# Grouped instance norm on one core: gamma's load and columns rebuilt, an early write and 60 no-ops removed

## The chip, the cores and the metric

The kernel runs on one core of one Trainium2 chip. The metric is the device time of one execution in microseconds (us); before the change its median is 626.75 us over 3 runs (626.71 to 626.87). The core has five engines that run side by side, each with its own instruction stream: TensorE (PE, with its weight loads shown as PEld), VectorE (DVE), ScalarE (ACT), GpSimd (POOL) and SyncE (SP). Transfers between the chip's main memory (HBM) and the on-chip memory (SBUF) are carried by 16 DMA engines. SyncE, ScalarE and GpSimd each issue transfers into a queue of their own; the 16 engines serve all queues.

## The reference

```python
def reference(x, gamma):                       # x: 4 x 8 x 16 x 256 x 256, gamma: 8 x 16
    mu = x.mean(axis=(3, 4), keepdims=True)
    var = ((x - mu) ** 2).mean(axis=(3, 4), keepdims=True)
    x_norm = (x - mu) / np.sqrt(var + 1e-5)
    out = x_norm * gamma[None, :, :, None, None]
    return out.astype(np.float32)
```

There are 4 x 8 x 16 = 512 channels of 65,536 numbers. Each is normalized by its own mean and variance and multiplied by one number of gamma. 134 MB are read and 134 MB are written.

## The kernel before

A channel is cut into S = 8 pieces of F = 8192 numbers, and a tile holds K = 16 channels: 128 partitions (8 neighbouring ones belong to a channel) by 8192 numbers, 4 MB. There are U = 32 tiles, and gamma repeats every NG = 8 tiles. Six slots of SBUF (AHEAD = 6, `xt`) hold tiles; each is loaded, normalized in place and stored from the same slot. So load u + 6 has to wait until store u has landed.

The order on each engine is the order of the code. The loads of the first six tiles are issued at once, tiles 1 and 3 on ScalarE's queue and 0, 2, 4 and 5 on SyncE's (lines 56 and 57). Later loads are SyncE's (line 136), all 32 stores are ScalarE's (line 134).

For a tile (lines 105 to 136) VectorE sums every partition (line 107) and ScalarE squares with a running sum (line 108); both wait for the load. One matmul with the constant matrix `navg` adds the 8 partitions of a channel, scales by -1/65536, and gives every partition of the channel the result (line 116, `ps`; in 4-byte floats it runs as two halves). VectorE forms the negative variance (`nvar`, line 117), ScalarE the root (`std`, line 121), VectorE the reciprocal (`rstd`, line 125) and its product with gamma (`scale`, line 127), which reads a column of `g_col`; then VectorE normalizes the tile (line 130), and ScalarE issues the store.

The column `g_col` has to hold, for each of the 8 tile kinds, gamma's value of each partition. Before the change it is made ahead of the loop. Gamma is loaded as one row of 128 numbers on one partition (`g_row`, line 55, GpSimd's queue). VectorE repeats each number 8 times (`g_rep`, line 83), 8 matmuls with a single 1 as the other operand turn the row into 8 columns (`g_ps`, line 88), and VectorE copies them to SBUF (line 94).

Three more things stand ahead of the loop. VectorE zeroes a small tile `touch`, and GpSimd's queue writes it to 16 rows of the output, 512 bytes each, in the place of tile 0 (lines 53 and 54); store 0 later overwrites it. ScalarE gets 60 no-ops behind its two loads (lines 59 and 60). A root over a constant (`root_eps`, line 78) has ScalarE load its table of functions early.

Of the kernel before, what the change touches and what calls it, by code (L numbers as in the profile page):

```python
# [1 line left out]

# [4 lines left out]

F32 = mybir.dt.float32
U8 = mybir.dt.uint8
ALU = mybir.AluOpType  # L10
ACTF = mybir.ActivationFunctionType
AX = mybir.AxisListType


@with_exitstack
def kernel(
    ctx: ExitStack,
    tc: tile.TileContext,
    x: bass.AP,
    gamma: bass.AP,  # L20
    out: bass.AP,
):
    nc = tc.nc
    B, G, C, H, W = x.shape
    P = nc.NUM_PARTITIONS
    HW = H * W
    n_ch = B * G * C
    S = 8
    K = P // S
    F = HW // S  # L30
    U = n_ch // K
    NG = (G * C) // K
    AHEAD = 6
    assert HW % S == 0 and (G * C) % K == 0

    xv = x.rearrange("b g c h w -> (b g c h w)").rearrange("(u p f) -> u p f", p=P, f=F)
    ov = out.rearrange("b g c h w -> (b g c h w)").rearrange("(u p f) -> u p f", p=P, f=F)
    gv = gamma.rearrange("g c -> (g c)")

    data = ctx.enter_context(tc.tile_pool(name="data", bufs=1))  # L40
    singles = ctx.enter_context(tc.tile_pool(name="singles", bufs=1))
    psum = ctx.enter_context(tc.tile_pool(name="psum", bufs=4, space=bass.MemoryType.PSUM))
    ctx.enter_context(tc.manual_schedule())

    slots = [data.tile([P, F], F32, name=f"xt{i}") for i in range(AHEAD)]

    def load(u, queue):
        queue.dma_start(out=slots[u % AHEAD][:], in_=xv[u])  # L48


    g_row = singles.tile([1, G * C], F32, name="g_row")
    touch = singles.tile([16, 128], F32, name="touch")
    nc.vector.memset(touch[:], 0.0)  # L53
    nc.gpsimd.dma_start(out=ov[0][0::S, 0:128], in_=touch[:])  # L54
    nc.gpsimd.dma_start(out=g_row[:], in_=gv[None, :])  # L55
    for u in range(AHEAD):
        load(u, nc.scalar if u in (1, 3) else nc.sync)

    for _ in range(60):
        nc.scalar.nop()  # L60

    eps_t = singles.tile([P, 1], F32, name="eps_t")
    nc.gpsimd.memset(eps_t[:], 1e-5)
    one = singles.tile([1, 1], F32, name="one")
    nc.gpsimd.memset(one[:], 1.0)
    navg = singles.tile([P, K, S], F32, name="navg")
    nc.gpsimd.memset(navg[:], -1.0 / HW)  # L67
    nc.gpsimd.affine_select(  # L68
        out=navg[:], in_=navg[:], pattern=[[-S, K], [0, S]], compare_op=ALU.is_ge,
        fill=0.0, base=0, channel_multiplier=1,  # L70
    )
    nc.gpsimd.affine_select(  # L72
        out=navg[:], in_=navg[:], pattern=[[S, K], [0, S]], compare_op=ALU.is_ge,
        fill=0.0, base=S - 1, channel_multiplier=-1,
    )
    navg_w = navg[:].rearrange("p k s -> p (k s)")
    root_eps = singles.tile([P, 1], F32, name="root_eps")
    nc.scalar.activation(out=root_eps[:], in_=eps_t[:], func=ACTF.Sqrt)  # L78
    g_rep = singles.tile([1, NG, K, S], F32, name="g_rep")
    g_ps = psum.tile([P, NG], F32, name="g_ps", bufs=1)  # L80
    g_col = singles.tile([P, NG], F32, name="g_col")

    nc.vector.tensor_copy(  # L83
        out=g_rep[:],
        in_=g_row[:].rearrange("o (n k) -> o n k", n=NG).unsqueeze(3).to_broadcast([1, NG, K, S]),
    )
    for n in range(NG):
        nc.tensor.matmul(  # L88
            out=g_ps[:, n : n + 1],
            lhsT=g_rep[:, n].rearrange("o k s -> o (k s)"),  # L90
            rhs=one[:],
            start=True, stop=True,
        )
    nc.vector.tensor_copy(out=g_col[:], in_=g_ps[:])  # L94

    junk = singles.tile([P, F], U8, name="junk")

    st = singles.tile([P, U, 2], F32, name="st")
    nvar = singles.tile([P, U], F32, name="nvar")
    std = singles.tile([P, U], F32, name="std")  # L100
    rstd = singles.tile([P, U], F32, name="rstd")
    scale = singles.tile([P, U], F32, name="scale")

    squares = []
    for u in range(U):
        t = slots[u % AHEAD]
        nc.vector.reduce_sum(out=st[:, u, 0:1], in_=t[:], axis=AX.X)  # L107
        square = nc.scalar.activation(  # L108
            out=junk[:], in_=t[:], func=ACTF.Square, accum_out=st[:, u, 1:2],
        )  # L110
        if u:

            tc.declare_no_dep(square.ins, squares[-1].ins, reason="junk, ordered by the root between")
        squares.append(square)
        ps = psum.tile([P, 2], F32, name="ps")
        nc.tensor.matmul(out=ps[:], lhsT=navg_w, rhs=st[:, u], start=True, stop=True)  # L116
        nc.vector.tensor_scalar(  # L117
            out=nvar[:, u : u + 1], in0=ps[:, 0:1], scalar1=ps[:, 0:1],
            scalar2=ps[:, 1:2], op0=ALU.mult, op1=ALU.add,
        )  # L120
        nc.scalar.activation(  # L121
            out=std[:, u : u + 1], in_=nvar[:, u : u + 1], func=ACTF.Sqrt,
            bias=eps_t[:], scale=-1.0,
        )
        nc.vector.reciprocal(out=rstd[:, u : u + 1], in_=std[:, u : u + 1])  # L125
        g = u % NG
        nc.vector.tensor_mul(  # L127
            out=scale[:, u : u + 1], in0=rstd[:, u : u + 1], in1=g_col[:, g : g + 1],
        )
        nc.vector.tensor_scalar(  # L130
            out=t[:], in0=t[:], scalar1=ps[:, 0:1], scalar2=scale[:, u : u + 1],
            op0=ALU.add, op1=ALU.mult,
        )
        nc.scalar.dma_start(out=ov[u], in_=t[:])
        if u + AHEAD < U:
            load(u + AHEAD, nc.sync)


# [1 line left out]
_INS = ['x', 'gamma']  # L140
_OUTS = [((4, 8, 16, 256, 256), 'float32')]


# [23 lines left out]
```

## Time and profile before

| what | value |
|---|---|
| median of the runs | 626.75 us (3 runs, 626.71 to 626.87) |
| span of the profiled execution | 624.9 us |
| HBM read, written | 134.22 MB, 134.23 MB, together 430 GB/s over the span |
| packets of the DMA engines | 9282, of which 1072 under 512 bytes |
| VectorE, sum of a tile (L107) | 8685 ns each, 32 times |
| VectorE, normalize a tile (L130) | 4550 ns each, 32 times |
| ScalarE, squares of a tile (L108) | 7030 ns each, 32 times |
| TensorE, half a matmul of the sums (L116) | 349 ns each, 64 |
| VectorE, repeat gamma (L83), copy the columns (L94) | 681 ns, 166 ns, once each |
| TensorE, half a matmul of gamma (L88) | 347 ns each, 16 |
| store, from issue to landing (L134) | 62.5 us median |
| load on SyncE's queue, on ScalarE's queue (L48) | 38.5 us, 31.5 us median |
| early write (L54), gamma's load (L55) | 9.1 us, 13.3 us |

The span is the time from the first to the last instruction that the profiler recorded in one execution; the runs' time has something around it. A row of a group of instructions gives how often it ran and how long one took. The time to landing counts from the issue of a transfer until its completion is signalled, the time in the queue behind others included. A chain of waits is followed back from the last instruction: at each step to what released it. In a table by stretches the times are counted from the start of the span, and the DMA share is the mean busy share of the 16 engines, where a packet counts in the stretch in which it starts. No-ops don't appear among the recorded instructions.

### The profile page before, as it was taken

The numbers are of one execution on the slowest core, as the hardware profiler recorded it, in microseconds if no ns is written. First come the engines' busy times: TensorE is split into PE (matmuls) and PEld (weight loads), VectorE is DVE, ScalarE is ACT, GpSimd is POOL, SyncE is SP. The second block draws the span as 40 slices with busy tenths as digits, with TensorE's granted clock in tenths as the row PEclk, the third lists the DMA queues.
The fourth block names the chain that finished last, engine by engine and source line by source line (L and its number), as shares of the span: only waits on it lengthen the run. The fifth ranks groups of instructions, "written<-read, shape, count | busy, mean of one in ns | idle before, by whom it ended". The sixth has DMA issues, their size and how long they took to land.

```text
span 624.9 us, 631 instructions
## 1 busy us (share of the span) xinstructions
PE 21.4 (3%) x80; PEld 19.5 (3%) x80; DVE 443.4 (71%) x163; ACT 238.8 (38%) x98; POOL 2.4 (0%) x11
## 2 busy tenths in 40 slices
PE   0200000000000000000000000000000000000000
PEld 0200000000000000000000000000000000000000
DVE  0588999999776687666786767867668676687730
ACT  0444444444443234432344423444224442244400
POOL 1000000000000000000000000000000000000000
DMA  8999999999999999999999999999999999999998
GB/s 370 436 426 430 422 434 436 436 436 437 432 424 433 436 436 424 436 436 434 436 436 432 422 436 436 434 426 436 436 434 436 436 434 419 436 436 434 426 436 369
DMA packets 9282, 268.46 MB, mean 430 GB/s; under 512 B 1072, under 2 KB 1088, under 8 KB 1088
## 3 DMA queue, kind: packets, MB, share of 16 engines
q10 hardware_dynamic: 4896, 142.61, 52.9%
q1 hardware_dynamic: 4320, 125.83, 46.8%
q0 software_dynamic: 64, 0.01, 0.0%
q14 instruction: 2, 0.02, 0.0%
HBM read 134.22 MB, written 134.23 MB: 430 GB/s over the span
## 4 chain that ended last, share of the span: by engine, by line
another core or an unknown queue 61%; DMA 17%; DVE 15%; SPq 1%; PE 1%; issue 0%; ACT 0%
DVE st L107 10%; DMA xt<-in_x_dram 10%; DMA out_dram<-xt 8%; DVE xt L130 5%; SPq L48 1%; PE ps L116 1%; ACT std L121 0%; DVE nvar L117 0%; DVE rstd L125 0%; DVE scale L127 0%
## 5 line engine op out<-in xcount | busy, mean ns | idle before, releaser
L107 DVE TENSOR_REDUCE st<-xt 128x1 f32<-128x8192 f32 x32 | 277.9, 8685 | 100.4 <-DMA xt<-in_x_dram 100.4
L108 ACT ACTIVATE junk<-xt 128x8192 uint8<-128x8192 f32 x32 | 225.0, 7030 | 275.1 <-DMA xt<-in_x_dram 231.9
L130 DVE TENSOR_SCALAR xt<-xt,ps,scale 128x8192 f32<-128x8192 f32 x32 | 145.6, 4550 | 1.2
L121 ACT ACTIVATE std<-nvar,eps_t 128x1 f32<-128x1 f32 x32 | 9.4, 294 | 79.6 <-DVE nvar L117 79.6
L116 PE MATMUL ps<-st,navg 128*128 128x2 f32 x64 | 17.9, 349 | 557.1 <-DVE st L107 557.1
L116 PEld LDWEIGHTS ps<-st,navg 128*128 128x128 f32 x64 | 16.0, 311 | 558.9 <-issue 558.9
L117 DVE TENSOR_SCALAR nvar<-ps 128x1 f32<-128x1 f32 x32 | 9.2, 287 | 23.8 <-PE ps L116 23.8
L125 DVE RECIPROCAL rstd<-std 128x1 f32<-128x1 f32 x32 | 5.2, 164 | 11.6 <-ACT std L121 11.6
L83 DVE COPY g_rep<-g_row 1x1024 f32<-1x1024 f32 x1 | 0.7, 681 | 14.3 <-DMA g_row<-in_gamma_dram 14.3
L108 ACT ACTIVATION_READ_ACCUMULATOR junk<-xt 128x1 f32 x32 | 6.0, 186 | 0.0
L127 DVE TENSOR_TENSOR scale<-rstd,g_col 128x1 f32<-128x1 f32 x32 | 5.1, 159 | 1.1
L88 PE MATMUL g_ps<-one,g_rep 1*128 1x1 f32 x16 | 3.5, 347 | 16.1 <-DVE g_rep L83 16.1
L88 PEld LDWEIGHTS g_ps<-one,g_rep 1*128 1x128 f32 x16 | 3.5, 325 | 16.1 <-issue 16.1
L94 DVE COPY g_col<-g_ps 128x8 f32<-128x8 f32 x1 | 0.2, 166 | 3.7 <-PE g_ps L88 3.7
L78 ACT ACT_TABLE_LOAD x1 | 1.3, 1283 | 1.7 <-PEq L151 1.7
L53 DVE MEMSET touch<- 16x128 f32 x1 | 0.2, 165 | 0.9 <-PEq L151 0.9
L54 POOL DMA_DIRECT2D out_dram<-touch x1 | 0.6, 619 | 0.8 <-DVE touch L53 0.8
L55 POOL DMA_DIRECT2D g_row<-in_gamma_dram x1 | 0.5, 487 | 0.0
L68 POOL TENSOR_SCALAR_AFFINE_SELECT navg<-navg 128x128 f32<-128x128 f32 x1 | 0.4, 400 | 0.1
L72 POOL TENSOR_SCALAR_AFFINE_SELECT navg<-navg 128x128 f32<-128x128 f32 x1 | 0.4, 399 | 0.1
L67 POOL MEMSET navg<- 128x128 f32 x1 | 0.2, 232 | 0.0
L78 ACT ACTIVATE root_eps<-eps_t 128x1 f32<-128x1 f32 x1 | 0.2, 203 | 0.0
(6 smaller groups left out, 0.6 us busy)
## 6 DMA issues: line engine op xcount, KB each, us to landing
out_dram<-xt ACTq DMA_DIRECT2D x32, 4096.0 KB, 62.5
xt<-in_x_dram SPq DMA_DIRECT2D x30, 4096.0 KB, 38.5
xt<-in_x_dram ACTq DMA_DIRECT2D x2, 4096.0 KB, 31.5
out_dram<-touch POOLq DMA_DIRECT2D x1, 8.0 KB, 9.1
g_row<-in_gamma_dram POOLq DMA_DIRECT2D x1, 0.5 KB, 13.3
```

The source lines that it names most:

```text
L48: queue.dma_start(out=slots[u % AHEAD][:], in_=xv[u])
L78: nc.scalar.activation(out=root_eps[:], in_=eps_t[:], func=ACTF.Sqrt)
L83: nc.vector.tensor_copy(out=g_rep[:], in_=g_row[:].rearrange("o (n k) -> o n k", n=NG).unsqueeze(3).to_broadcast([1, NG, K, S]),)
L88: nc.tensor.matmul(out=g_ps[:, n : n + 1], lhsT=g_rep[:, n].rearrange("o k s -> o (k s)"), rhs=one[:], start=True, stop=True,)
L107: nc.vector.reduce_sum(out=st[:, u, 0:1], in_=t[:], axis=AX.X)
L108: square = nc.scalar.activation(out=junk[:], in_=t[:], func=ACTF.Square, accum_out=st[:, u, 1:2],)
L116: nc.tensor.matmul(out=ps[:], lhsT=navg_w, rhs=st[:, u], start=True, stop=True)
L117: nc.vector.tensor_scalar(out=nvar[:, u : u + 1], in0=ps[:, 0:1], scalar1=ps[:, 0:1], scalar2=ps[:, 1:2], op0=ALU.mult, op1=ALU.add,)
L121: nc.scalar.activation(out=std[:, u : u + 1], in_=nvar[:, u : u + 1], func=ACTF.Sqrt, bias=eps_t[:], scale=-1.0,)
L125: nc.vector.reciprocal(out=rstd[:, u : u + 1], in_=std[:, u : u + 1])
L127: nc.vector.tensor_mul(out=scale[:, u : u + 1], in0=rstd[:, u : u + 1], in1=g_col[:, g : g + 1],)
L130: nc.vector.tensor_scalar(out=t[:], in0=t[:], scalar1=ps[:, 0:1], scalar2=scale[:, u : u + 1], op0=ALU.add, op1=ALU.mult,)
```

## The change

Gamma is loaded as it lies in memory, 8 rows of 16 numbers (64 bytes) on 8 partitions, by ScalarE's queue between loads 1 and 3. GpSimd issues no transfer any more. The early write with its memset and the 60 no-ops are gone. GpSimd makes an 8 x 8 unit matrix `eye` in place of the single 1. Within the loop, behind the sum of tile 0 on VectorE, the rows are repeated 8 times each (8 partitions x 128 numbers), one matmul with the unit matrix gives all 8 columns at once, and VectorE copies them.

```diff
@@ -48,21 +47,21 @@
-    g_row = singles.tile([1, G * C], F32, name="g_row")
-    touch = singles.tile([16, 128], F32, name="touch")
-    nc.vector.memset(touch[:], 0.0)
-    nc.gpsimd.dma_start(out=ov[0][0::S, 0:128], in_=touch[:])
-    nc.gpsimd.dma_start(out=g_row[:], in_=gv[None, :])
+
+    g_rows = singles.tile([NG, K], F32, name="g_rows")
     for u in range(AHEAD):
         load(u, nc.scalar if u in (1, 3) else nc.sync)
-
-    for _ in range(60):
-        nc.scalar.nop()
+        if u == 1:
+            nc.scalar.dma_start(out=g_rows[:], in_=gamma)
 
     eps_t = singles.tile([P, 1], F32, name="eps_t")
     nc.gpsimd.memset(eps_t[:], 1e-5)
-    one = singles.tile([1, 1], F32, name="one")
-    nc.gpsimd.memset(one[:], 1.0)
+    eye = singles.tile([NG, NG], F32, name="eye")
+    nc.gpsimd.memset(eye[:], 0.0)
+    nc.gpsimd.affine_select(
+        out=eye[:], in_=eye[:], pattern=[[-1, NG]], compare_op=ALU.not_equal,
+        fill=1.0, base=0, channel_multiplier=1,
+    )
@@ -76,22 +75,16 @@
-    g_rep = singles.tile([1, NG, K, S], F32, name="g_rep")
+    g_rep = singles.tile([NG, K, S], F32, name="g_rep")
     g_ps = psum.tile([P, NG], F32, name="g_ps", bufs=1)
     g_col = singles.tile([P, NG], F32, name="g_col")
 
-    nc.vector.tensor_copy(
-        out=g_rep[:],
-        in_=g_row[:].rearrange("o (n k) -> o n k", n=NG).unsqueeze(3).to_broadcast([1, NG, K, S]),
-    )
-    for n in range(NG):
+    def gamma_columns():
+        nc.vector.tensor_copy(out=g_rep[:], in_=g_rows[:].unsqueeze(2).to_broadcast([NG, K, S]))
         nc.tensor.matmul(
-            out=g_ps[:, n : n + 1],
-            lhsT=g_rep[:, n].rearrange("o k s -> o (k s)"),
-            rhs=one[:],
-            start=True, stop=True,
+            out=g_ps[:], lhsT=g_rep[:].rearrange("n k s -> n (k s)"), rhs=eye[:], start=True, stop=True,
         )
-    nc.vector.tensor_copy(out=g_col[:], in_=g_ps[:])
+        nc.vector.tensor_copy(out=g_col[:], in_=g_ps[:])
@@ -105,6 +98,8 @@
         nc.vector.reduce_sum(out=st[:, u, 0:1], in_=t[:], axis=AX.X)
+        if u == 0:
+            gamma_columns()
         square = nc.scalar.activation(
             out=junk[:], in_=t[:], func=ACTF.Square, accum_out=st[:, u, 1:2],
         )
```

More of the change, by code (lines that the diff above doesn't have):

```diff
@@ L33 @@
     AHEAD = 6
-    assert HW % S == 0 and (G * C) % K == 0
+    assert HW % S == 0 and C == K and NG == G
     xv = x.rearrange("b g c h w -> (b g c h w)").rearrange("(u p f) -> u p f", p=P, f=F)
     ov = out.rearrange("b g c h w -> (b g c h w)").rearrange("(u p f) -> u p f", p=P, f=F)
-    gv = gamma.rearrange("g c -> (g c)")
     data = ctx.enter_context(tc.tile_pool(name="data", bufs=1))
```

## The prediction, as put on record before the result

> **What bounds the kernel now.** I read the share of busy time first, then the transfers, then the chain of waits, and last the stretches between the issues of the later loads.
>
> ```profile
> span 624.9 us, 631 instructions
> PE 21.4 (3%) x80; PEld 19.5 (3%) x80; DVE 443.4 (71%) x163; ACT 238.8 (38%) x98; POOL 2.4 (0%) x11
> DMA  8999999999999999999999999999999999999998
> q10 hardware_dynamic: 4896, 142.61, 52.9%
> q1 hardware_dynamic: 4320, 125.83, 46.8%
> q0 software_dynamic: 64, 0.01, 0.0%
> q14 instruction: 2, 0.02, 0.0%
> ```
>
> VectorE is busy for 71% of the span and nothing else comes near, except the DMA engines, at 9 tenths or more in all slices but the first and the last. q10 is ScalarE's queue (loads 1 and 3, all stores), q1 is SyncE's, q0 GpSimd's. q10 and q1 add up to 99.7% of the 16 engines' span: the transfers set the time, and a saving elsewhere is worth nothing unless it gives them work earlier.
>
> The chain of waits, in order of time:
>
> ```profile
> 0.80 21.80 DMA xt<-in_x_dram
> 22.62 8.70 DVE st L107
> 31.45 0.57 PE ps L116 x2
> 32.05 0.30 DVE nvar L117
> 33.10 4.55 DVE xt L130
> 37.65 8.61 DVE st L107
> ...
> 112.34 47.23 DMA out_dram<-xt
> ...
> 178.96 0.33 SPq L48
> ...
> 198.30 0.33 SPq L48
> ```
>
> VectorE works on the first six tiles without a pause, up to 112.3 us; then the chain is a wait on SyncE's queue every 19.34 us. That is one load and one store of 4 MB each. Stretches cut at SyncE's issues of later loads show where the transfers fall short of that pace (columns: stretch, its length, busy time and count of each engine, granted clock, DMA share, GB/s):
>
> ```profile
> 0.00:22.60 22.60, 3.54 (x16) 3.48 (x16) 1.01 (x3) 1.49 (x2) 2.40 (x11) 1.00 0.94 395
> 41.90:62.34 20.44, 1.12 (x4) 1.01 (x4) 18.38 (x7) 10.81 (x6) 0.00 (x0) 1.00 0.95 410
> 62.34:81.66 19.32, 0.56 (x2) 0.50 (x2) 17.84 (x8) 7.62 (x4) 0.00 (x0) 1.00 1.01 434
> 139.76:159.60 19.84, 0.56 (x2) 0.50 (x2) 16.37 (x7) 7.61 (x4) 0.00 (x0) 1.00 1.01 436
> ```
>
> From 159.62 to 546.72 SyncE issues 20 loads after the first, one each 19.355 us; I use 19.36. The kernel moves 32 such pairs: 32 x 19.36 = 619.5 us. The span is 624.9, so 5.4 us is all that is not plain streaming. Of it, 22.60 - 19.36 = 3.24 lies before tile 0 has landed: 0.80 of entry, 1.0 until the first packet (the packet view is empty up to 1.7 us and has the first five between 1.7 and 1.9), and 1.4 of slow start. 20.44 - 19.36 = 1.08 is lost where the first stores begin, 19.84 - 19.36 = 0.48 in the stretch to 159.60, and 624.9 - 623.95 = 0.95 is the exit after SyncE's last wait. These come to 5.75; the 0.3 too much is in the other stretches, a little under 19.36 a pair. So the change cannot touch more than about 1.4 + 1.08 + 0.48 = 3.0 us, 0.5% of the time, on the side of gain.
>
> **The change part by part.**
>
> *GpSimd's two small transfers go.* They are all of q0: 64 packets, 0.0% of the 16 engines' span, so under 0.05% x 624.9 = 0.31 us on an engine. The early write landed 9.1 us after its issue and gamma 13.3 us; nobody on the chain of the end waited for either. The packets lie between those of the first loads, on engines that are never idle then, so their whole time comes back: 0 to -0.31 us. I take -0.1, since the share is printed as 0.0.
>
> *Gamma goes to ScalarE's queue.* One more issue between loads 1 and 3: such an issue took 0.40 to 0.46 us there, so load 3 is issued at about 1.7 us in place of 1.23, and the table load (1.72 to 3.00) and root_eps end 0.45 us later. Load 3's first packet is not due before load 1 has left the queue, near 22 us, and ScalarE's next work starts at 22.62: cover of some 19 us for both. The transfer is 8 rows; beside 8 data packets I count 8 for completion (q0's 64 are 32 of data and completion for each of two transfers over 16 engines), a quarter of q0's: at most 2 on an engine in place of 4, so 0 to +0.16 us. I take +0.05. It stands behind load 1 and so lands near 22.3 us, not at 15.3; its reader comes at 31.3, cover 9 us. SyncE's queue keeps its order, and GpSimd is free to start its constants about 1.6 us earlier; it gains an 8 x 8 memset and one select (at most 0.1 and 0.40 us by its 128 x 128 rows), needed at 31 us. VectorE's memset of the early write (0.17 us, at 0.89) goes and was on no path.
>
> *The columns of gamma move behind the sum of tile 0.* The 0.68 us copy, 16 half matmuls (3.54 us) and 0.17 us copy that filled VectorE's wait from 15.3 to 19.9 us go. In their place, on VectorE after 31.31: a copy of 128 elements on each of 8 partitions. From the two copies, 681 ns at 1024 elements and 166 at 8, an element is 0.51 ns, so 0.23 us. Then a matmul of two halves: from the end of the sum to nvar took 32.05 - 31.31 = 0.74 us with the matmul within. Then the 0.17 us copy. TensorE holds tile 0's own matmul right behind, and that costs another 0.56. Tile 0's nvar is late by 0.23 + 0.56 + hand-over, 0.85 us; wholly in series it would be 0.23 + 0.74 + 0.17 = 1.14. Behind it wait on VectorE the rest of tile 0 and tiles 1 to 5, each 0.85 late; on ScalarE the root of tile 0, and behind that the store's issue and Square of tile 1. Store 0 is issued at about 38.5, not 37.68. It is late for the engines only when loads 1 and 3 have left ScalarE's queue, at 22.60 + 19.36 = 41.96, less the 1.0 us from issue to packet: 40.9. Cover left: 2.4 us. If that were gone, SyncE's queue still holds loads 4 and 5 (all four of its first issues are made by 2.77), and the same engines run on with those. Store 5, issued at 112.34, lands 47.23 us later where a pair takes 19.36: it queues for 27 us, so 0.85 us is lost there too. Cost: 0.
>
> *The 60 no-ops.* The table load ends at 3.00 and root_eps starts at 3.01, while loads 1 and 3 were issued by 1.69: there is no stretch of ScalarE for them, except under the table load. Time of their own: 0. But they are program that has to be fetched. The page has 2 instruction packets of 0.01 MB each; the packet view puts one between 150 and 160 us, the other between 195 and 202. The first stretch is the late one, 0.48 us over the pace; the second (198.30 to 217.66, 19.36 us) is not late. Without the no-ops, and with 28 fewer matmuls and weight loads, either fetch may fall away (-0.48 at best, less where the next slowest engine is close), or only move to another engine (0, or up to +0.48 there). I take -0.25, about half. The Trainium skill (page "Runtime: NRT & Kernel Launch", section "Instruction fetch mechanics") has a crossing of a fetch boundary as mostly hidden; by it this term would be 0 and the time 626.75. The 19.84 us stretch speaks against it, the second fetch for it.
>
> *The early write goes.* If it prepared the engines for the stores, its price appears at 41.9 us. No row has a first store without it. Below: 0, as 1.08 us is lost in that stretch though the write had landed 30 us before. Above: the dearest start in the trace, that of the first loads, 3.24 - 0.80 = 2.44 us with the latency in it. I take +0.05, nearest to the row of the same place.
>
> **The sum**, on the profiled execution: -0.1 + 0.05 + 0 - 0.25 + 0.05 = -0.25 us, a span of 624.65. The median of the runs shown, 626.75, stands 1.85 above the span; I keep that and get 626.5. What a measurement of this kernel can tell from no change is about 0.2%, 1.25 us: under 625.5 is faster, over 628.0 slower. My forecast is no change.
>
> **The rivals.**
>
> *The first store stalls without the early write (slower).* One mechanism at one place: the stretch from 41.9, where all 16 engines write the output for the first time. Both queues share the engines, so a stall there stops the loads too and is never made up. For it: the write went to every eighth row of tile 0, 16 rows for 16 engines, and something there costs 1.08 us even so. Against: the stores to fresh tiles in the stretches after 62.34 lose nothing. Its price is 1.4 us (the slow start without entry and latency) to 2.44: 627.9 to 628.9, say 628.4. It decides from a stall of 1.5 us. The Trainium skill (page "HBM Reference", section "Latency") gives an HBM access 0.2 us on average and 2 us at high load; with that 2 us the time would be 628.5. No run here shows such a figure.
>
> *The small software transfers cost more than their packets (faster).* If the early write and gamma on q0 make part of the slow start, and a part of the 1.08 us too, dropping them gives back half of 1.4 + 1.08, 1.2 us, beside the -0.25: 625.3. For it: they lie in the stretch with 395 GB/s. Against: they landed at 10.5 and 15.3 us, and the first packets of any run start cold.
>
> *The new wait bites.* Were gamma to land only with load 3, near 42 us, VectorE would stand still for 10.7 us behind its copy. Store 5 would be issued at 123.0 and still queue for 16 us; between 42 and 50 us the engines would work on loads 4 and 5 alone. That ends at 626.5 to 627.4, the upper end if 0.85 us does come through: no change.
>
> **How the numbers follow.** The forecast has 0.65 (its own range 625.9 to 627.3: the ends of the fetch and of the small packets); the new wait 0.08, also no change; the slower rival 0.17; the faster one 0.10. So faster 0.10, same 0.73, slower 0.17. Outside the sum's own range lies 0.27 of rivals with a price, so the range goes to 625.3 below and 628.4 above, which leaves out about half of each.
>
> **What would show it.** In the changed kernel: no q0 row, or no packets in it; the first stretch to tile 0's landing still near 22.6 us (0.1 shorter; much shorter is the faster rival); tile 0's nvar near 32.9 and store 0 near 38.5; the stretch from 41.9 near 20.4 (22 or more is the slower rival); the pace 19.36 after it; the instruction packets gone from the stretch to 159.6, and that stretch 19.4. Wrong would be a pace other than 19.36, a pause in both queues at once, or a time that moves while the span does not.

## The result, and the profile after

The changed kernel takes 629.39 us in the middle of 8 runs (627.32 to 630.77), the kernel before beside it 626.84 (626.71 to 627.47, 8 runs): a ratio of 1.0038 (95% interval 1.0027 to 1.0049), 2.55 us slower. More than the middle has moved: the kernel before keeps within 0.8 us, the changed one spreads over 3.4, and 7 of its 8 runs lie over 628.5, which the kernel before passed in none of its runs below (highest 627.59). I count runs over 628.5 us for each experiment for that reason. The profiled execution of the changed kernel was the longest of its runs, 630.77 us with a span of 629.0; the difference, 1.8 us, is that of before.

The page of the changed kernel:

```profile
span 629.0 us, 600 instructions
PE 18.4 (3%) x66; PEld 16.5 (3%) x66; DVE 442.7 (70%) x162; ACT 238.8 (38%) x98; POOL 1.5 (0%) x10
DMA  8999999999999999999999999999999999999996
q10 hardware_dynamic: 4912, 142.61, 52.5%
q1 hardware_dynamic: 4320, 125.83, 46.7%
q14 instruction: 2, 0.02, 0.0%
```

GpSimd's queue q0 is gone, ScalarE's q10 has 16 packets more, the bytes of the two large queues are the same. The DMA engines are still what is busy, but the last slice has fallen from 8 to 6 tenths. The chain of waits, in order of time:

```profile
0.80 21.76 DMA xt<-in_x_dram
22.59 8.69 DVE st L100
31.27 0.13 DVE g_rep L83
31.54 0.56 PE g_ps L84 x2
32.10 0.53 PE ps L111 x2
32.66 0.30 DVE nvar L112
33.70 4.55 DVE xt L125
...
112.95 49.58 DMA out_dram<-xt
...
162.58 0.33 SPq L47
...
181.92 0.33 SPq L47
...
375.77 0.33 SPq L47
...
395.29 0.33 SPq L47
...
453.72 0.33 SPq L47
...
473.21 0.33 SPq L47
```

Gamma's copy and matmul now stand in the chain between the sum and nvar, and all that follows on VectorE is 0.6 us late, as 112.95 beside 112.34 shows. The pace of SyncE's queue is the news: 181.92 - 162.58 = 19.34 us as before, but 395.29 - 375.77 = 19.52 and 473.21 - 453.72 = 19.49 in the second half, where the kernel before had 19.36 to its end.

The same by stretches (length, busy time of the engines, clock, DMA share, GB/s), cut at SyncE's issues, and then the tail in steps of 2 us:

```profile
0.00:22.60 22.60, 0.00 (x0) 0.00 (x0) 0.01 (x1) 1.50 (x3) 1.46 (x10) 1.00 0.94 394
41.90:65.06 23.16, 1.12 (x4) 1.01 (x4) 20.80 (x10) 11.61 (x6) 0.00 (x0) 1.00 0.99 407
142.68:162.56 19.88, 0.56 (x2) 0.50 (x2) 16.98 (x7) 10.54 (x4) 0.00 (x0) 1.00 1.01 436
375.76:395.28 19.52, 0.56 (x2) 0.50 (x2) 13.89 (x6) 7.46 (x4) 0.00 (x0) 1.00 1.00 430
622.00:624.00 2.00, 0.00 (x0) 0.00 (x0) 0.00 (x0) 0.00 (x0) 0.00 (x0) 1.00 0.65 279
624.00:626.00 2.00, 0.00 (x0) 0.00 (x0) 0.00 (x0) 0.00 (x0) 0.00 (x0) 1.00 0.15 66
626.00:628.00 2.00, 0.00 (x0) 0.00 (x0) 0.00 (x0) 0.00 (x0) 0.00 (x0) 1.00 0.08 33
```

The kernel before, in the same steps of its tail:

```profile
622.00:624.00 2.00, 0.00 (x0) 0.00 (x0) 0.00 (x0) 0.00 (x0) 0.00 (x0) 1.00 0.19 82
624.00:626.00 2.00, 0.00 (x0) 0.00 (x0) 0.00 (x0) 0.00 (x0) 0.00 (x0) 1.00 0.04 8
```

This is where the time is. After 624 us most engines are done, and what remains, 66 and then 33 GB/s, is the work of one or two of the 16. The trace's packet records say the same: of the 16 completion packets of the last store, 14 come between 623.5 and 624.5 us and two at 627.7; in the kernel before all 16 lie between 622.7 and 623.6. So the changed kernel as a whole is 0.7 to 0.9 us late, two engines fell another 3 us or more behind, and the kernel ends when the last engine does.

The records show how the order of the engines' packets changed, too. A row of a tile, 32 KB, takes an engine 1.213 us, and in the kernel before each engine takes one packet of q1 and one of q10 in turn throughout. What the queues moved between 22.2 and 24.4 us, after loads 0 and 1, first before, then changed (packets, MB, share of the 16 engines):

```profile
q10 hardware_dynamic: 17, 0.52, 55.2%
q1 hardware_dynamic: 12, 0.36, 37.9%
```

```profile
q1 hardware_dynamic: 12, 0.39, 41.4%
q10 hardware_dynamic: 19, 0.26, 27.9%
```

q10 has 19 packets but half the bytes: 8 of 32 KB and 11 short ones. On 8 engines the packet of 64 bytes stands in the turn where load 3's first row would have been, and then its completion packet takes the next one. These engines give q1 two large packets more before q10 goes on, and from then on these 8 are out of step with the other 8: at the same point of time their q10 is one row further back.

### The profile page after: what moved, and what is told of

It reads as the page before. It is cut to its first block, busy times and chain, and to the rows that moved or that the text cites. A ratio compares the mean times of both kernels' runs of the same rounds, so it can differ in the third digit from the quotient of the medians.

```text
span 629.0 us, 600 instructions
## 1 busy us (share of the span) xinstructions
PE 18.4 (3%) x66; PEld 16.5 (3%) x66; DVE 442.7 (70%) x162; ACT 238.8 (38%) x98; POOL 1.5 (0%) x10
## 3 DMA queue, kind: packets, MB, share of 16 engines
q1 hardware_dynamic: 4320, 125.83, 46.7%
## 4 chain that ended last, share of the span: by engine, by line
another core or an unknown queue 61%; DMA 17%; DVE 15%; SPq 1%; PE 1%; issue 0%; ACT 0%
DVE st L100 10%; DMA xt<-in_x_dram 9%; DMA out_dram<-xt 8%; DVE xt L125 5%; SPq L47 1%; PE ps L111 1%; ACT std L116 0%; DVE nvar L112 0%; DVE rstd L120 0%; DVE scale L122 0%; PE g_ps L84 0%; DVE g_rep L83 0%
```

## The experiments

Theory A: the first store of each engine is dear without the early write. B: gamma's short packets in ScalarE's queue put half of the engines out of step. C: the fetch of the program moved. D, E and F come below. Medians and ratios are against the kernel before, run beside it on the same chip (626.82, 627.15, 626.86 and 627.03 us on the four chips used). The early write and the no-ops leave the output as it is, and so do the extra loads and copies, which nobody reads.

**The two things dropped.** Early write put back into the changed kernel, and taken from the kernel before:

```diff
+    touch = singles.tile([16, 128], F32, name="touch")
+    nc.vector.memset(touch[:], 0.0)
+    nc.gpsimd.dma_start(out=ov[0][0::S, 0:128], in_=touch[:])
```

> The changed kernel with the early write put back, gamma still on ScalarE's queue. Theory A (the first store of each engine is dear without an early write, and that is the whole loss): back to 626.8 us, the stretch up to SyncE's first later load 62.4 again. Theory B (gamma's short packets on 8 of the 16 engines take turns of ScalarE's queue and put those engines out of step): the loss stays, 628.5 to 630, first later load still near 65. Both in parts: about 628.

Measured: 627.82 us, ratio 1.0021 (1.0012 to 1.0029), 3 of 11 runs over 628.5.

> The kernel before without the early write and nothing else. Theory A: slower by the loss, 628 to 629.4, with the stretch of the first stores 1.5 us or more longer. Theory B: 626.8 and up to 0.7 us more (the packet records of the changed kernel show the first packet beside a store 0.65 us longer on each engine), 627.5 at most.

Measured: 626.80 us, ratio 0.9999 (0.9991 to 1.0008), none of 11 over 628.5. Theory A falls: the kernel before does without the early write. That putting it back gains anything in the changed kernel is not shown either: the ratio was 1.0021 with it, and the changed kernel without it came to 1.0022 on the last chip (below).

```diff
-    for _ in range(60):
-        nc.scalar.nop()
```

> The kernel before without the 60 no-ops and nothing else. Theories A and B: 626.8 within 0.3 us. Theory C (the fetch of ScalarE's program moves and costs more): slower by 0.5 us or more, with an instruction packet at another place than 155 and 199 us.

Measured: 626.83 us, ratio 0.9999 (0.9990 to 1.0007), none of 11 over 628.5, and instruction packets in the same places, 155.8 and 199.4 us. Theory C falls. The built program explains it: ScalarE has 102 instructions (65 operations, 34 transfers, the table load, two branches) with the no-ops in the source and 102 without. They are not built at all, so the kernel before never had 60 no-ops to fetch.

**Gamma by GpSimd.** The changed kernel with the 8 rows on GpSimd's queue:

```diff
+    nc.gpsimd.dma_start(out=g_rows[:], in_=gamma)
     for u in range(AHEAD):
         load(u, nc.scalar if u in (1, 3) else nc.sync)
-        if u == 1:
-            nc.scalar.dma_start(out=g_rows[:], in_=gamma)
```

> The changed kernel with gamma's 8 rows issued by GpSimd, so that no short packets stand in ScalarE's queue; no early write, no no-ops. Theory B: loads and stores in step again, first later load near 62.4 to 63, time 626.5 to 627.2. Theory A: the first stores still pay, 0.7 us more or all of the loss: 627.5 to 629.4.

Measured: 629.41 us, ratio 1.0031 (1.0017 to 1.0045); three runs at 626.6 to 627.0, six at 628.7 to 630.1. The profiled one was of the three, with all engines in step, store 0 issued at 38.29 us and the first later load at 62.21. So B, which foretold 627 for all, is not the whole, and A was gone already: something else in the change makes most runs 2 to 3 us longer and spares some. What was left was the columns behind the sum of tile 0 (theory D, then E: store 0 is issued 0.6 us later) or the rows, the unit matrix and the shorter program of TensorE (F).

**The columns alone.** In the kernel before without early write and no-ops, its own copy, 8 matmuls and copy put into a function that is called behind the sum of tile 0:

```diff
         nc.vector.reduce_sum(out=st[:, u, 0:1], in_=t[:], axis=AX.X)
+        if u == 0:
+            gamma_columns()
```

> The kernel before without the early write and the no-ops (626.8 us when each was left out alone), with its own one-row gamma and its 8 matmuls moved behind the sum of tile 0: store 0 is issued some 4.5 us later, near 42.2, after ScalarE's queue has run empty at 41.9. Theory D (a later store 0 puts loads and stores out of step; in the changed kernel it is 0.6 us late): slower, 628 to 630, with a spread over 1 us. Theory B (only short packets in ScalarE's queue do): 626.8, spread as before.

Measured: 626.95 us, ratio 0.9996 (0.9988 to 1.0005), none of 11 over 628.5, with store 0 issued at 41.62 us and the first later load at 65.69. D falls in its plain form: 4 us late costs nothing.

The earlier kernel with gamma by GpSimd, with the same call put ahead of the loop:

> The changed kernel with gamma's 8 rows issued by GpSimd, as in the earlier run, and now the copy, the one matmul and the copy ahead of the loop, so that store 0 is issued near 37.7 again. Theory D: 626.8 in all runs. If the 8 rows on GpSimd's queue or the shorter program of TensorE are the cause instead: 629 in most runs, as that earlier run had it.

Measured: 627.17 us, ratio 0.9999 (0.9990 to 1.0008), none of 11 over 628.5, store 0 at 37.70 us. The rows, the unit matrix and the short program are all in it, and the long runs are gone. That speaks against F.

**The short packets alone.** In the kernel before without early write and no-ops, one more load:

```diff
         load(u, nc.scalar if u in (1, 3) else nc.sync)
+        if u == 1:
+            nc.scalar.dma_start(out=extra[:], in_=gamma)
```

> The kernel before without the early write and the no-ops, plus one transfer that nobody reads: gamma's 8 rows on ScalarE's queue between loads 1 and 3 (8 engines get a short packet). Theory B: slower by 1 to 2.5 us with SyncE's first later load near 65. Theory D alone: 626.8 us, even if the first later load comes later.

Measured: 627.82 us, ratio 1.0011 (1.0002 to 1.0020), all 11 runs between 627.62 and 628.05, store 0 at 37.56, the first later load at 65.20. The loss that theory B foretold was 1 to 2.5 us; it is 0.7, and clear all the same: every run lies above every run of the kernel before on this chip (highest 627.56). The same with 16 rows of 32 bytes (`gamma.rearrange("g (a b) -> (g a) b", a=2)`):

> As the one with 8 extra rows, but 16 rows of 32 bytes, so that all 16 engines get a short packet and keep step with each other while ScalarE's queue as a whole falls back by two packets. Theory B in the form that the engines lose step with each other: 626.8 to 627.2. Theory B in the form that stores lose step with loads on an engine: as slow as with 8 rows or slower.

Measured: 627.04 us, ratio 0.9998 (0.9990 to 1.0007), none of 11 over 628.5, the highest 627.57. Its queues between 22.2 and 24.4 us:

```profile
q1 hardware_dynamic: 28, 0.88, 93.2%
q10 hardware_dynamic: 27, 0.00, 0.7%
```

Here q10 moves nothing but short packets: all 16 engines give up the turn, and ScalarE's queue falls back as a whole. The first later load comes as late as with 8 rows, at 64.85 us, and it costs nothing that can be told. What costs is that 8 engines do it and 8 don't. The packet records hint at the place: between 35 and 50 us, where the first stores begin, the 32 KB packets took 0.85 us an engine more than 1.213 us each with 16 rows, 0.77 in the kernel before without the early write, and 1.56 with 8 rows. It is a hint only: the same sum is 1.14 and 1.06 in two kernels that lose nothing (gamma by GpSimd with the columns ahead of the loop, and the next experiment). B holds, in its first form, at 0.7 us by the ratio (0.1 to 1.3).

**The moment of store 0.** The first try put two copies of an unused tile behind the sum of tile 0:

> The kernel before without the early write and the no-ops, with two short copies of a tile nobody uses behind the sum of tile 0 on VectorE: store 0 is issued near 38.3 us in place of 37.7, as in the changed kernel, and nothing else differs. Theory E (at that moment store 0 reaches some engines before and others after ScalarE's queue runs empty, and single engines fall behind for the rest of the run): most runs at 629 to 630, some at 626.7. Theory F (the 8 rows, the unit matrix or the shorter program of TensorE are behind it): all runs at 626.7 to 627.5.

Measured: 627.22 us, ratio 1.0002 (0.9993 to 1.0010). It tells nothing: the copies ran while VectorE waited for the matmul, and store 0 was issued at 37.60.

The other way round, six copies of 1024 numbers behind the columns in the kernel with gamma by GpSimd, that kernel again on the same chip, and the copies in the changed kernel itself:

```diff
         if u == 0:
             gamma_columns()
+            for _ in range(6):
+                nc.vector.tensor_copy(out=pad[:], in_=pad[:])
```

> The changed kernel with gamma's 8 rows issued by GpSimd, and six more copies of an unused tile on VectorE behind the columns: store 0 is issued some 4 us later, near 42.4, clear of the moment when ScalarE's queue runs empty. Theory E: no run near 629.6 any more, all at 626.7 to 627.5. Theory F: most runs at 629 to 630, as the same kernel without the copies.

> The changed kernel with gamma's 8 rows issued by GpSimd once more, unchanged, on the chip of the other runs of this call: 626.6 in some runs and 629 to 630 in the others, if that did not hang on the chip (theories E and F alike). All runs near 627.2 would mean that the other chip made the difference.

> The changed kernel itself with the six copies behind the columns, store 0 near 42.4 us. Theory E: the part of the loss that hangs on store 0's moment goes, what the short packets in ScalarE's queue cost alone stays: 627.6 to 628.1 with little spread, as with the 8 extra rows. Theory F: still 629 to 630.

Measured: with gamma by GpSimd and store 0 at 42.03 us, 627.09, ratio 1.0002 (0.9993 to 1.0010), none of 11 over 628.5. Without the copies, store 0 at 38.22: 628.79, ratio 1.0025 (1.0014 to 1.0035), 7 of 12 over 628.5. The changed kernel with the copies, store 0 at 42.16: 627.41, ratio 1.0005 (0.9996 to 1.0014), 1 of 11 over 628.5. So the kernel with gamma by GpSimd gets 1.7 us faster by 4 us of work put into it, on one chip. For the changed kernel itself the two times come from different chips (ratio 1.0005 with the copies, 1.0038 and 1.0022 without). E holds against F.

Then store 0 alone, in the kernel before without early write and no-ops, with copies where nothing covers them:

```diff
+        if u == 0:
+            for _ in range(2):        # 4 in the second kernel
+                nc.vector.tensor_copy(out=pad[:], in_=pad[:])
         nc.vector.tensor_scalar(
             out=t[:], in0=t[:], scalar1=ps[:, 0:1], scalar2=scale[:, u : u + 1],
```

> The kernel before without the early write and the no-ops, with two copies of an unused tile right ahead of the normalizing of tile 0 on VectorE, where nothing covers them: store 0 is issued near 38.3 us in place of 37.65. (The earlier try lay in the shadow of the matmul, and store 0 stayed at 37.6.) Theory E (the moment of store 0 decides): most runs 628.5 to 630, as with gamma's 8 rows on GpSimd and the columns in the loop. Theory F: all at 626.7 to 627.5.

> As the one with store 0 near 38.3, with four copies: store 0 near 39.0 us, its first packets expected from 40.0 us on, in the midst of the last packets of loads 2 and 3. Theory E: slow runs here too, perhaps more than at 38.3. Theory F: all at 626.7 to 627.5.

Measured: store 0 at 38.12 us gives 627.39, ratio 1.0009 (0.9998 to 1.0020), 3 of 11 over 628.5; store 0 at 38.88 gives 629.31, ratio 1.0039 (1.0022 to 1.0056), 9 of 12 over 628.5, the longest 633.32. Nothing of gamma is changed in these two. At 38.12 most runs had been expected over 628.5, and 3 of 11 were; 38.88 is the clear case. With all kernels that send no short packets through ScalarE's queue, the share of runs over 628.5 goes with the moment of store 0: 0 of 44 at 37.60 to 37.72, 3 of 11 at 38.12, 13 of 21 at 38.22 to 38.29, 9 of 12 at 38.88, and 0 of 22 at 41.62 and 42.03.

The profile of the kernel with store 0 at 38.88 (one of its 629.47 us) shows the mark of the changed kernel, first in its chain, then in its tail:

```profile
278.41 0.33 SPq L48
...
297.87 0.33 SPq L48
```

```profile
622.00:624.00 2.00, 0.00 (x0) 0.00 (x0) 0.00 (x0) 0.00 (x0) 0.00 (x0) 1.00 0.46 197
624.00:626.00 2.00, 0.00 (x0) 0.00 (x0) 0.00 (x0) 0.00 (x0) 0.00 (x0) 1.00 0.11 49
```

A pair takes 297.87 - 278.41 = 19.46 us, and 49 GB/s are left after 624. The packet records of this execution, put in chains by what follows on what, show its birth (start in us, queue, and the time taken where it is not 1.21):

```
14 engines, as:   38.79 q1   40.00 q10 (1.40)   41.41 q1 (1.74)   43.14 q10         44.35 q1
one engine:       38.84 q1   40.05 q10          41.27 q1 (2.32)   43.58 q1 (1.56)   45.14 q10
another:          38.90 q1   40.11 q10          41.33 q1 (2.65)   43.98 q1 (1.49)   45.46 q10
```

On two engines q1 got two turns in a row at 41.3, the two on which q10's last packet of load 3 had ended first: store 0 had not yet come for them. Their first packet took 2.3 to 2.7 us in place of 1.7, 0.7 to 1.0 us more than the others over these packets, and they go on a packet out of step. Their chains then lose another 2 us or so each up to the end, mostly 0.05 to 0.35 at a time on the first load packet behind the end of a store; of the others most lose nothing after 150 us.

The packet records of the other profiles bear this out, execution by execution. An odd engine is here one that gave q1 two turns in a row at store 0's start while the others of its group gave one (where 8 engines were already out of step by short packets, the other 8 are the group).

| kernel profiled | store 0 at, us | odd engines | time of this execution, us |
|---|---|---|---|
| before, and six variants without short packets on ScalarE's queue | 37.60 to 38.29 | 0 of 16 | 626.7 to 627.6 |
| 8 extra rows | 37.56 | 0 of 8 | 627.88 |
| copies ahead of normalizing, two | 38.12 | 1 of 16 | 628.71 |
| changed, with early write | 38.32 | 1 of 8 | 628.53 |
| changed, again (below) | 38.32 | 1 of 8 | 628.07 |
| copies ahead of normalizing, four | 38.88 | 2 of 16 | 629.47 |
| changed, first profile | 38.28 | 2 of 8 | 630.77 |

In all five profiles with odd engines they are the ones of their group whose load packet at 41.2 to 41.5 us began first. In the changed kernel the two began at 41.38 and 41.48 and moved store 0's first row at 44.8 and 45.0; the other six began at 41.50 or later and moved it at 43.2 to 43.4. In these five the dividing line lies 2.5 to 3.2 us after store 0's issue: an engine that took up that packet sooner did not have the store yet, and one that took it up later had it.

Being out of step is not enough to go on losing. With store 0 at 42.03 us three engines moved its first row at 48.5 to 48.7, a turn after the other 13 (46.7 to 47.1); they kept that distance, and the execution took 626.74 us. The changed kernel with store 0 at 42.16 split 9 to 7 instead of 8 to 8, and that execution, 628.92 us, did go on losing. Why a packet after the end of a store is longer on an odd engine in one case and not in the other is not settled.

**A version without either fault, and the change again.** Gamma's rows first on ScalarE's queue, ahead of load 1, and the columns ahead of the loop:

```diff
+    nc.scalar.dma_start(out=g_rows[:], in_=gamma)
     for u in range(AHEAD):
         load(u, nc.scalar if u in (1, 3) else nc.sync)
-        if u == 1:
-            nc.scalar.dma_start(out=g_rows[:], in_=gamma)
...
+    gamma_columns()
...
-        if u == 0:
-            gamma_columns()
```

> The changed kernel with gamma's 8 rows first on ScalarE's queue, ahead of load 1, and the columns ahead of the loop. The short packets are gone before the loads are in step, and store 0 is back near 37.7. Theories B and E: 626.8 to 627.2, no slow runs. Load 1 is issued 0.4 us later; were that to put the loads out of step, 627.5 to 628.

> The changed kernel once more, unchanged, beside the others: 629 to 629.6 in the middle. If it comes near 627.4, as with store 0 four us late on another chip, the share of the loss that hangs on store 0's moment is not settled.

Measured: 626.94 us, ratio 1.0000 (0.9991 to 1.0008), none of 11 over 628.5, with gamma landed at 2.4 us. Store 0 was issued at 35.31 us, not near 37.7, because tile 0 had landed 2.3 us sooner, so it came well before ScalarE's queue ran empty. The changed kernel on this chip: 628.36, ratio 1.0022 (1.0013 to 1.0030), 4 of 11 over 628.5; that is less than the 629 to 629.6 expected, and the size of the loss, 1.4 us here and 2.55 first, is not the same in both sets of runs. The version with gamma first is as fast as the kernel before, without GpSimd's transfers, and none was found that beats it. The tail of its profile has no late engine:

```profile
622.00:624.00 2.00, 0.00 (x0) 0.00 (x0) 0.00 (x0) 0.00 (x0) 0.00 (x0) 1.00 0.12 49
624.00:626.00 2.00, 0.00 (x0) 0.00 (x0) 0.00 (x0) 0.00 (x0) 0.00 (x0) 1.00 0.00 0
```

## Why the prediction was wrong

It forecast no change, 626.5 us; the time is 629.39, above its range (625.3 to 628.4) too.

- **What bounds the kernel** was right: the DMA engines, 19.36 us a pair. But the prediction reckoned with the 16 engines as one, and the loss is one of single engines against the rest.
- **The columns behind the sum of tile 0: the step that failed.** The delay was read rightly (nvar forecast at 32.9, measured 32.66; store 0 forecast at 38.5, measured 38.28). "Cover left: 2.4 us" and, were it gone, "the same engines run on with those", cost 0, was wrong twice. The cover of 2.4 us was worked out from 1.0 us between issue and first packet, as the first loads have it on engines with nothing else to do, and from the end of load 3 on the last engine, 41.96 us. In the profiles the first engine needed store 0 at 41.2 to 41.5 us, and the store was there for an engine only 2.5 to 3.2 us after its issue; where the queue had run empty on all engines, its first row moved 3.9 and 4.7 us after the issue (45.55 for 41.62, 46.71 for 42.03). So there was hardly any cover left, and runs grow long from 38.12 us on, 0.45 us after the old moment. And an engine that runs on with the other queue alone, while others don't, is not free: in the kernel with store 0 at 38.88 it lost 0.7 to 1.0 us at once and went on losing. Measured: 1.7 us between store 0 at 38.22 and at 42.03 on one chip, 2.4 us (ratio 1.0039) for store 0 at 38.88 alone. The prediction had thought that cover only runs out for all engines at once; then, as the runs at 42 us show, it does cost nothing.
- **Gamma on ScalarE's queue** was mis-sized: the packets' own time was taken, 0 to +0.16 us, and not the turns that they take from the large packets on 8 of the 16 engines. That came to 0.7 us (0.1 to 1.3), shown apart from the rest. The other 1.8 of the 2.55 us is what is left for the moment of store 0; it is in line with the 1.7 and 2.4 measured apart, but this split of the changed kernel is a difference and was not measured on one chip (on the last chip the whole loss was 1.4).
- **GpSimd's two transfers**, -0.1: not to be told from nothing. The first stretch stayed at 22.6 us, 394 GB/s after 395.
- **The no-ops and the fetch**, -0.25: wrong, 0. The no-ops build no instruction, and both instruction packets are still there, at 156.6 and 212.1 us; the stretch of the first took 19.88 us after 19.84.
- **The early write**, +0.05: right in size, ratio 0.9999 (0.9991 to 1.0008) without it, though an effect of 0.05 us can't be told from none.
- **The slower rival** had the direction and the place, the first stores, but not the mechanism, and its price ended at 628.9 us. Its mark was badly chosen: "22 or more" in the stretch from 41.9. The changed kernel has 23.16 there, yet the kernels with 16 extra rows and with the columns alone have their first later load as late, 64.85 and 65.69 us, and lose nothing; when a store lands says which queue had the turns, not what was lost. The tail would have been the better mark. The pace, which the prediction did name as a sign of being wrong, was one in the first profile (19.52 for 19.36), but it is no sure one: in the later profile of the changed kernel, an execution of 628.07 us, it stays at 19.36 in the second half.
- **The faster rival** fell, and **the new wait** did not come: gamma landed in time (its completion packets are at 24.3 to 24.6 us, its reader at 31.2), and VectorE's copy followed its sum without a pause. Two waits in the prediction are about 1 us too short and change nothing: store 5 queues for 47.23 - 19.36 = 27.9 us and not 27, and in the new wait for 17.2 and not 16.

## What to carry to other kernels

Where the DMA engines set the time, a small transfer costs its turn and not its bytes: send it ahead of the stream, or over all 16 engines alike, and not over half of them between two large loads. Cover in such a kernel is to be reckoned for the engine whose queue runs empty first, with the time from issue to packet as it is between busy engines. Here a store that arrived just when its queue ran empty was worse than one well before or well after. When a time spreads more than it did, look at the tail: if the rate there falls to one or two engines' share, single engines have lost step, and the place to look is where some of them took another turn than the rest.

## What the runs showed that was not expected

- In the changed kernel a late engine did not come back. By the completion packets of its loads, the last engine is 0.4 us behind the third last at 314 us and 2.7 us at the last load, 587.75 after 585.04, though all of them wait for the same issues of SyncE.
- The first instruction packet of the later stretches, at 144 to 160 us, costs its engine the same in every profile: 0.31 us, and the large packet behind it takes 0.53 us longer if it is a load and 0.35 if it is a store. What it costs the kernel differs. SyncE's pace in its stretch was 19.84 us before, 19.85 without the early write, 20.48 in the first try at delaying store 0 and 20.65 with gamma by GpSimd run again, but 19.35 with store 0 at 42.03, for 19.36 elsewhere: 0 to 1.3 us. The Trainium skill (page "Runtime: NRT & Kernel Launch", section "Instruction fetch mechanics") has the crossing of a fetch boundary as mostly hidden; the 19.35 us agrees with that, the others do not. Why the stretch can lose more than the 0.84 us of the one engine is not settled.
